# Square, value and score products in other groups: a decoder step on one core

## The chip, the cores and the metric

One core of a Trainium2 chip runs the kernel. The metric is the time of one execution on the device in microseconds (us). Matrix products run on TensorE (PE), and the other compute engines are VectorE (DVE), ScalarE (ACT) and GpSimd (POOL); SyncE (SP) issues most transfers. Each engine works through its own list of instructions in order, and waits on semaphores for the others.

## The reference

One inference step of a one-layer decoder over 512 prompt tokens and 8 samples of 4 tokens, 1024 wide, all in fp32. Cut to what matters:

```python
def rmsnorm(x, g):
    return x * rsqrt(mean(x * x, -1) + EPS) * g

# both groups
h = rmsnorm(x, norm_mix_g) @ w_in          # -> ua va | q k v | qi ki wi
a = gelu(ua) * (tril(gm_ws) @ layernorm(gelu(va)) + gm_bs)
# prompt: per query the 128 best of index_scores(qi, wi, ki), causal
# samples: the 256 best of 2048 cached tokens (pages of 128) and the 4 new ones
b = softmax(q @ k_sel.T / 8) @ v_sel
x = x + concat(a, b) @ w_out
x = x + mem_attend(rmsnorm(x, norm_mem_g), mk, mv) @ mem_wo
xn = rmsnorm(x, norm_ffn_g)
# experts: 8 heads, 16 best of 128 x 128 keys, chosen rows of two tables
x = x + sum(softmax(top16) * gelu(u_tab[eid] . xn) * v_tab[eid])
return rmsnorm(x, final_norm_g), ...       # and keys, values, memory keys and values
```

## The kernel before

Activations stand with features on the partitions: `xT[p, kt, token]`, eight tiles of 128 features. A weight product is made of three products in a rounded fp32 format (`mm3`, lines 249 to 251: high x high, high x low, low x high). The two parts of a weight tile are split by ACT (line 213, the cast) and DVE (line 217, the rest); the parts of an activation by lines 192 and 193.

The program goes through a front stage (first norm, projections `wA`, masks by sorting the indexing scores, prompt attention, the selection for the samples and their attention, the memory), then two halves of the tokens (256 prompt tokens, and 256 with the 32 sample tokens: 288 columns). Each half has `wO`, a norm, `wMQ`, memory attention, `wMO`, a norm, `wP`. In the trace the first half's wO ends about 350 us, the second half's wO runs from 402 to 440, wMO from 440 to 460 and from 515 to 540. The experts follow, from about 570 us.

The order of the instructions on each engine is that of a scheduler, which lays the program out by its own estimate of times; the program only names dependencies, priorities by order of writing, and `issue_after(x)`, under which what is written comes behind x.

Three places are edited.
- `squares4` (line 139) adds up the squares of a norm. ACT squares a tile (line 141); of every four tiles, tile c's columns are summed by a product with ones into partitions 32c to 32c+31 of an accumulator (line 147). It is called from `folded` (first norm, two accumulators, 272 columns each) and from `residual` (line 528), which adds an output tile to `xT` (line 527, DVE) and squares it. A norm needs eight products for each accumulator; the squares' buffers are four (`bufs=4`). Then `turned` and `row_factors` (lines 116 to 126 and 185 to 187) make the factors of the rows.
- `attend` has the prompt's attention in four blocks of 128 queries. `values` sums over b + 1 blocks of keys (line 886), for two groups of heads, which write partitions 0 to 63 and 64 to 127 of one bank.
- `sample_keys` multiplies each sample's queries with its cached keys (line 1496). Each page holds its keys in a 16-element slice per partition group; four slices (e), two pages (f), two halves of the rows (o, each with an accumulator of its own) and two halves of the output (c). ACT copies the accumulators (line 1500), and the next pages are fetched. The samples' value products are line 1553.

An fp32 product, as these three are, shows in the trace as two passes on PE.

Of the kernel before, what the change touches and what calls it, by code (L numbers as in the profile page):

```python
# [18 lines left out]
P = 128  # L19
NP = 512  # L20
NS = 32
NT = NP + NS
KT = 8
# [28 lines left out]
class Kernel:  # L52
# [83 lines left out]
                                  start=kt == 0 and b == 0, stop=kt == KT - 1, skip_group_check=True)  # L136


    def squares4(self, room, x, kt, st, w):
        sq = self.t(room, [P, w], tag="nsqs", bufs=4)  # L140
        self.nc.scalar.square(sq, x)
        self.sq4 = [sq] if kt % 4 == 0 else self.sq4 + [sq]
        if kt % 4 == 3:
            n = w // len(st)
            for i, ps in enumerate(st):
                for c, q in enumerate(self.sq4):
                    self.nc.tensor.matmul(ps[c * NS : c * NS + NS, :n], self.ones[:, :NS], q[:, i * n : i * n + n],
                                          start=kt == 3, stop=kt == KT - 1, skip_group_check=True)


    def turned(self, room, st, w):
# [693 lines left out]
    def attend(self, pw, qT, kT, v_n, mb):  # L845
        nc = self.nc
        keep = {}

        def scores(b, r):
            L = (b + 1) * P  # L850
            pss = [self.pst("pa") for g in range(2)]
            for g, ps in enumerate(pss):
                o = g * 64
                nc.tensor.matmul(ps[:, :L], qT[o : o + 64, r, b * P : b * P + P], kT[o : o + 64, :L], start=True, stop=True)
            return [soft(b, ps[:, :L]) for ps in pss]

        def soft(b, ps):
            sm = self.t(pw, [P, 512], tag="sm", bufs=2 * self.SKEW + 2)[:, : (b + 1) * P]
            mx = self.t(pw, [P, 1], tag="mx", bufs=4)
            nc.vector.tensor_tensor_reduce(sm, ps, mb[b], 0.125, NEG, ALU.add, ALU.max, mx)  # L860
            nm = self.t(pw, [P, 1], tag="nm", bufs=4)
            nc.vector.tensor_scalar(nm, mx, -1.0, None, ALU.mult)
            z = self.t(pw, [P, 1], tag="z", bufs=4)
            nc.scalar.activation(sm, sm, AF.Exp, bias=nm, accum_out=z)
            rz = self.t(pw, [P, 1], tag="rz", bufs=4)
            nc.vector.reciprocal(rz, z)
            nc.scalar.activation(sm, sm, AF.Copy, scale=rz)
            return sm

        def values(b, r, sms):  # L870
            L = (b + 1) * P
            if r == 0:
                keep["y"] = self.pst("pc")
            yb = keep["y"]
            for g, sm in enumerate(sms):
                if r % 2 == 0:
                    keep[g] = self.t(pw, [P, 4, 2, P], tag=f"pts{g}", bufs=self.PTB)
                pt = self.pst("pb")
                for s in range(b + 1):
                    nc.tensor.transpose(pt[:, s * P : s * P + P], sm[:, s * P : s * P + P], self.ident)  # L880
                nc.scalar.copy(keep[g][:, : b + 1, r % 2, :], pt[:, :L].rearrange("p (s t) -> p s t", t=P))
            if r % 2:

                for s in range(b + 1):
                    for g in range(2):
                        nc.tensor.matmul(yb[g * 64 : g * 64 + 64, (r - 1) * P : (r + 1) * P], v_n[:, s, g * 64 : g * 64 + 64],
                                         keep[g][:, s, :, :], start=s == 0, stop=s == b, skip_group_check=True)
            if r == 3:

                nc.scalar.copy(qT[:, :, b * P : b * P + P], yb.rearrange("p (r t) -> p r t", r=4))  # L890
                self.attended = b + 1


        ahead = []
        for b in range(4):
            while b > self.masked:
                yield 1.0
            for r in range(4):
                ahead.append((b, r, scores(b, r)))
                if len(ahead) > self.SKEW:  # L900
                    values(*ahead.pop(0))
                yield self.ATT * (b + 1) / 2
        for x in ahead:
            values(*x)
            yield self.ATT * 2
# [551 lines left out]
    def sample_keys(self, s1, s2):  # L1457
        nc = self.nc

        qb = self.s_qb = self.t(s2, [P, 8, 2, 4, 4])  # L1460
        nc.vector.memset(qb, 0.0)
        for g in range(2):
            r = slice(g * 64, g * 64 + 64)
            for q in range(4):
                nc.vector.tensor_scalar(qb[r, :, g, q], self.s_q[r, q].rearrange("p (b t) -> p b t", t=4), 0.125, None, ALU.mult)

        qs = self.t(s2, [P, 4, 8, 16])
        self.s_room = Room(qs.rearrange("p e b q -> p (e b q)"))
        ps = self.pst("pb")
        for e in range(4):  # L1470
            perm = self.t(s1, [P, P], tag="qst", bufs=2)
            nc.vector.tensor_copy(perm.rearrange("p (u g d) -> p u g d", u=4, g=2),
                                  self.ident.rearrange("p (g e d) -> p e g d", g=2, e=4)[:, e].unsqueeze(1).to_broadcast([P, 4, 2, 16]))
            nc.tensor.matmul(ps[:, e * P : e * P + P], perm, self.s_q.rearrange("p r t -> p (r t)"), start=True, stop=True)
        for e in range(4):
            nc.scalar.activation(qs[:, e].rearrange("p b (r t) -> p r b t", r=4), ps[:, e * P : e * P + P].rearrange("p (r b t) -> p r b t", r=4, b=8),
                                 AF.Copy, scale=0.125)

        own = self.t(s2, [P, 4])
        nc.vector.tensor_reduce(own, self.ident.rearrange("p (r c d) -> p c r d", r=2, d=16), AX.XY, ALU.add)  # L1480
        yield 1.0
        while not self.indexed:
            yield 1.0
        S = [self.t(s1, [P, 4, 512], tag="S8", bufs=2) for _ in range(2)]
        self.s_S = [S[b // 4][:, b % 4, :] for b in range(8)]
        for b in range(8):
            q4 = self.t(s2, [P, 4, 64], tag="q4", bufs=2)
            nc.vector.tensor_tensor(q4.rearrange("p e (c q) -> p e c q", c=4), qs[:, :, b].unsqueeze(2).to_broadcast([P, 4, 4, 16]),
                                    own.unsqueeze(1).unsqueeze(3).to_broadcast([P, 4, 4, 16]), ALU.mult)

            pair = [self.pst("pb") for _ in range(2)]
            for e in range(4):
                for f in range(2):
                    for o, ps in zip((0, 64), pair):
                        for c in range(2):
                            nc.tensor.matmul(ps[c * 64 : c * 64 + 64, f * P : f * P + P], q4[o : o + 64, e],
                                             self.kv[b][o : o + 64, 2 * c + f, e * P : e * P + P], start=e == 0 and f == 0, stop=e == 3,
                                             skip_group_check=True, tile_position=(o, c * 64))
            for r, ps in enumerate(pair):
                nc.scalar.copy(self.s_S[b].rearrange("p (m r f x) -> p r f m x", m=4, r=2, f=2)[:, r],  # L1500
                               ps[:, : 2 * P].rearrange("p (f m x) -> p f m x", f=2, m=4))
            self.fetch_kv(s2)
            yield 4.0 * self.SK
        self.keyed = True
# [366 lines left out]
```

## Time and profile before

| what | value |
|---|---|
| time, median of 3 (lowest to highest) | 1797.16 us (1795.39 to 1797.25) |
| the profiled execution: its time, its span | 1793.41 us, 1791.7 us |
| PE busy | 1675.7 us, 94% |
| DVE busy | 1482.9 us, 83% |
| ACT busy | 863.2 us, 48% |
| POOL busy | 503.6 us, 28% |
| PE in line 147 (96 passes), line 886 (80), line 1496 (512): median pass | 406, 380, 270 ns |

Busy is the time in which at least one instruction of the engine runs. A pass's own length contains the filling and draining of the array, which overlap the next one; so the distance from a start to the next start is what a pass costs. The shares are means over stages with different limits, and are to be read stage by stage.

### The profile page before, as it was taken

What the parts mean: (1) busy time and instruction counts of PE and PEld (TensorE: products, weight loads), DVE (VectorE), ACT (ScalarE), POOL (GpSimd) and SP (SyncE); (2) the same over time, 40 slices, a digit from 0 to 9 for tenths busy, and PEclk for the clock granted to TensorE, in tenths of its full rate; (3) what the DMA queues carried; (4) which work ended last, traced back from release to release, by engine and by line L of the source; (5) the groups of instructions that cost most, each with busy time, mean ns of one, the idle gap of its engine ahead of it and who ended that gap; (6) DMA issues with size and microseconds to landing.
All of it is one profiled execution on the core that took longest, in us unless ns stands there. A gap on an engine that the chain in (4) does not pass through costs nothing. (4 is left out here: it accounts for less than half of the span.)

```text
span 1791.7 us, 30106 instructions
## 1 busy us (share of the span) xinstructions
PE 1675.7 (94%) x10494; PEld 1476.6 (82%) x10494; DVE 1482.9 (83%) x3654; ACT 863.2 (48%) x1584; POOL 503.6 (28%) x437
## 2 busy tenths in 40 slices
PE   7999889989996999799999999999999999999995
PEld 5879757778875889789899998888788888888884
DVE  4586899755759999998999887799898888878897
ACT  4355765764543434674675575233343333333333
POOL 3000123120000054223224222334333534345343
PEclk9999769989998999999999999999999999999997
DMA  5423425445752599789779789799998999999986
GB/s 179 128 83 98 126 85 199 140 166 170 238 172 90 169 345 329 267 316 334 256 269 322 242 306 316 267 353 333 360 356 300 375 357 328 349 334 324 358 305 231
DMA packets 195207, 460.36 MB, mean 257 GB/s; under 512 B 17976, under 2 KB 98616, under 8 KB 193648
## 3 DMA queue, kind: packets, MB, share of 16 engines
q1 hardware_dynamic: 132928, 241.63, 39.7%
q0 software_dynamic: 53072, 207.71, 32.5%
q10 hardware_dynamic: 9056, 9.11, 1.6%
q8 instruction: 82, 1.34, 0.3%
q14 instruction: 69, 0.57, 0.1%
HBM read 416.11 MB, written 42.05 MB: 256 GB/s over the span
## 5 line engine op out<-in xcount | busy, mean ns | idle before, releaser
L251 PE MATMUL t<-t,t 128*128 128x384 f32 (+3 forms) x2544 | 867.9, 346 | 12.5 <-DVE t L217 12.2
L250 PE MATMUL t<-t,t 128*128 128x384 f32 (+3 forms) x2544 | 867.6, 343 | 0.0
L249 PE MATMUL t<-t,t 128*128 128x384 f32 (+3 forms) x2544 | 779.9, 346 | 17.6 <-ACT t L213 15.1
L213 ACT CAST t<-t 128x1024 fp32r<-128x1024 f32 (+4 forms) x512 | 418.2, 841 | 716.8 <-PE t L250 475.8
L217 DVE TENSOR_TENSOR t<-t,t 128x1024 fp32r<-128x1024 f32 (+4 forms) x512 | 488.6, 965 | 140.0 <-ACT t L213 136.3
L251 PEld LDWEIGHTS t<-t,t 128*128 128x128 f32 x2544 | 485.0, 191 | 66.4 <-DVE t L217 15.7
L249 PEld LDWEIGHTS t<-t,t 128*128 128x128 f32 x2544 | 485.0, 191 | 61.2 <-ACT t L213 20.3
L250 PEld LDWEIGHTS t<-t,t 128*128 128x128 f32 x2544 | 485.4, 191 | 38.4 <-issue 5.7
L1276 POOL DMA_INDIRECT t<-in_u,t x160 | 201.7, 1260 | 499.0 <-DVE t L1736 305.0
L1276 POOL DMA_INDIRECT t<-in_v,t x160 | 215.5, 1347 | 298.0 <-DVE t L1741 233.9
L1741 DVE SCALAR_TENSOR_TENSOR t<-t,t,t 128x1024 f32<-128x1024 f32 x160 | 204.9, 1281 | 4.5 <-DMA t<-in_v,t 3.6
L1736 DVE SCALAR_TENSOR_TENSOR t<-t,t 128x1024 f32<-128x1024 f32 x160 | 193.8, 1219 | 8.7 <-DMA t<-in_u,t 8.6
L1081 ACT ACTIVATE t<-t 128x512 f32<-128x512 f32 x96 | 96.6, 1148 | 19.3 <-DMA wd<-t 18.5
L1276 POOL DMA_INDIRECT t<-in_cK,t x32 | 32.3, 1009 | 212.1 <-PE t L1359 146.5
L1217 DVE TENSOR_TENSOR t<-t,t 128x352 f32<-128x352 f32 x128 | 66.6, 521 | 6.2 <-DMA t<-wd 4.0
L1097 ACT ACTIVATE t<-t 128x384 f32<-128x384 f32 x128 | 62.3, 487 | 11.8 <-PE t L251 9.2
L1071 ACT ACTIVATE t<-t,t 128x128 f16<-128x128 f16 x192 | 58.2, 395 | 10.1 <-DVE t L1067 7.4
L1078 PE MATMUL t<-t,t 128*128 128x128 f16 x384 | 51.8, 221 | 9.4 <-ACT t L1081 8.8
L1276 POOL DMA_INDIRECT t<-in_cV,t x32 | 34.2, 1069 | 72.0 <-PE t L1553 45.1
L695 ACT ACTIVATE t<-t,t 128x384 f32<-128x384 f32 x64 | 42.7, 666 | 24.4 <-DVE t L692 20.3
L1079 PE MATMUL t<-t,t 128*128 128x128 f16 x384 | 49.7, 221 | 0.4 <-DVE t L1073 0.3
L1079 PEld LDWEIGHTS <-t 128*128 128x128 f16 x384 | 36.7, 98 | 10.6 <-issue 10.1
(400 smaller groups left out, 1471.2 us busy)
## 6 DMA issues: line engine op xcount, KB each, us to landing
t<-in_uT SPq DMA_DIRECT2D x128, 512.0 KB, 5.8
t<-in_v SPq DMA_DIRECT2D x128, 512.0 KB, 6.2
wd<-t POOLq DMA_DIRECT2D x11, 2048.0 KB, 9.2
t<-wd SPq DMA_DIRECT2D x32, 704.0 KB, 7.9
gd<-t SPq DMA_DIRECT2D x56, 192.0 KB, 5.3
t<-gd SPq DMA_DIRECT2D x56, 192.0 KB, 7.6
t<-in_wA SPq DMA_DIRECT2D x19, 512.0 KB, 4.0
t<-in_wO SPq DMA_DIRECT2D x16, 512.0 KB, 4.0
```

The costliest lines, as they stand in the source:

```text
L213: self.nc.scalar.copy(hi, x)
L217: self.pin_v = self.nc.vector.tensor_tensor(lo, x, hi, ALU.subtract)
L249: mm(out, ah, bh, start=first, stop=False)
L250: mm(out, ah, bl, start=False, stop=False)
L251: self.pin = mm(out, al, bh, start=False, stop=last)
L1079: nc.tensor.matmul(o, oj[:, x, :], ol[:, x, :], start=False, stop=True)
L1081: nc.scalar.activation(wb[:, :, t : t + 4].rearrange("p i t -> p t i"), ps.rearrange("p (t i) -> p t i", t=4), AF.Copy, scale=1.0 / 2048.0)
L1097: nc.scalar.activation(G, ps, AF.Gelu_apprx_tanh)
L1217: nc.vector.tensor_tensor(q(w)[:, : 4 * NB - 1], self.wp[:, :, i % 4, :], q(G)[:, : 4 * NB - 1], ALU.mult)
L1276: self.nc.gpsimd.indirect_dma_start(out=out, out_offset=None, in_=src, in_offset=bass.IndirectOffsetOnAxis(ap=ix, axis=0))
L1736: nc.vector.scalar_tensor_tensor(r, r, 1.0, hf, ALU.mult, ALU.mult, accum_out=a[:, k : k + 1])
L1741: nc.vector.scalar_tensor_tensor(acc, r, a[:, k : k + 1], acc, ALU.mult, ALU.add)
```

## The change

`together` takes products written as functions. It issues the last of them first, and the others under `issue_after` of it. `squares4` hands it the four products of an accumulator, `values` the two products of one block of keys. In `sample_keys` the loop over f is gone: one product of 256 columns covers both pages, and the number of products falls from 256 to 128.

```diff
--- before.py
+++ after.py
@@ -136,6 +136,13 @@
                                   start=kt == 0 and b == 0, stop=kt == KT - 1, skip_group_check=True)
 
 
+    def together(self, products):
+        first = products[-1]()
+        with self.tc.issue_after(getattr(first, "ins", first)):
+            for p in products[:-1]:
+                p()
+
+
     def squares4(self, room, x, kt, st, w):
         sq = self.t(room, [P, w], tag="nsqs", bufs=4)
         self.nc.scalar.square(sq, x)
@@ -143,9 +150,9 @@
         if kt % 4 == 3:
             n = w // len(st)
             for i, ps in enumerate(st):
-                for c, q in enumerate(self.sq4):
-                    self.nc.tensor.matmul(ps[c * NS : c * NS + NS, :n], self.ones[:, :NS], q[:, i * n : i * n + n],
-                                          start=kt == 3, stop=kt == KT - 1, skip_group_check=True)
+                self.together([lambda c=c, q=q: self.nc.tensor.matmul(ps[c * NS : c * NS + NS, :n], self.ones[:, :NS], q[:, i * n : i * n + n],
+                                                                      start=kt == 3, stop=kt == KT - 1, skip_group_check=True)
+                               for c, q in enumerate(self.sq4)])
 
 
     def turned(self, room, st, w):
@@ -882,9 +889,9 @@
             if r % 2:
 
                 for s in range(b + 1):
-                    for g in range(2):
-                        nc.tensor.matmul(yb[g * 64 : g * 64 + 64, (r - 1) * P : (r + 1) * P], v_n[:, s, g * 64 : g * 64 + 64],
-                                         keep[g][:, s, :, :], start=s == 0, stop=s == b, skip_group_check=True)
+                    self.together([lambda g=g: nc.tensor.matmul(yb[g * 64 : g * 64 + 64, (r - 1) * P : (r + 1) * P], v_n[:, s, g * 64 : g * 64 + 64],
+                                                                keep[g][:, s, :, :], start=s == 0, stop=s == b, skip_group_check=True)
+                                   for g in range(2)])
             if r == 3:
 
                 nc.scalar.copy(qT[:, :, b * P : b * P + P], yb.rearrange("p (r t) -> p r t", r=4))
@@ -1490,12 +1497,11 @@
 
             pair = [self.pst("pb") for _ in range(2)]
             for e in range(4):
-                for f in range(2):
-                    for o, ps in zip((0, 64), pair):
-                        for c in range(2):
-                            nc.tensor.matmul(ps[c * 64 : c * 64 + 64, f * P : f * P + P], q4[o : o + 64, e],
-                                             self.kv[b][o : o + 64, 2 * c + f, e * P : e * P + P], start=e == 0 and f == 0, stop=e == 3,
-                                             skip_group_check=True, tile_position=(o, c * 64))
+                for o, ps in zip((0, 64), pair):
+                    for c in range(2):
+                        nc.tensor.matmul(ps[c * 64 : c * 64 + 64, : 2 * P].rearrange("p (f x) -> p f x", f=2), q4[o : o + 64, e],
+                                         self.kv[b][o : o + 64, 2 * c : 2 * c + 2, e * P : e * P + P], start=e == 0, stop=e == 3,
+                                         skip_group_check=True, tile_position=(o, c * 64))
             for r, ps in enumerate(pair):
                 nc.scalar.copy(self.s_S[b].rearrange("p (m r f x) -> p r f m x", m=4, r=2, f=2)[:, r],
                                ps[:, : 2 * P].rearrange("p (f m x) -> p f m x", f=2, m=4))
```

Lines behind 139 have numbers higher by 7 in the changed kernel (by 6 behind the score products): line 147 is 153, 886 is 892, 1496 is 1502, 249 to 251 are 256 to 258.

PE, the second half's wMO, where its last square product stands (t_6586 is the accumulator of the squares, t_58 the ones, t_7009 and t_7056 accumulators of the next weight tiles). Before:

```order
L251 MATMUL t_7009<-t_6768,t_7006 128x288
L249 MATMUL t_7009<-t_6768,t_7005 128x288
L249 MATMUL t_7056<-t_6768,t_7052 128x288
L250 MATMUL t_7056<-t_6769,t_7052 128x288
L250 MATMUL t_7009<-t_6769,t_7005 128x288
L251 MATMUL t_7009<-t_6768,t_7006 128x288
L147 MATMUL t_6586<-t_5273,t_58 32x288
L249 MATMUL t_7009<-t_6768,t_7005 128x288
L251 MATMUL t_7056<-t_6768,t_7053 128x288
```

Of the changed kernel (the accumulator of the squares is t_6458 here, the next weight tiles' are t_6881 and t_6928):

```order
L258 MATMUL t_6881<-t_6640,t_6878 128x288
L256 MATMUL t_6881<-t_6640,t_6877 128x288
L256 MATMUL t_6928<-t_6640,t_6924 128x288
L257 MATMUL t_6928<-t_6641,t_6924 128x288
L257 MATMUL t_6881<-t_6641,t_6877 128x288
L258 MATMUL t_6881<-t_6640,t_6878 128x288
L153 MATMUL t_6458<-t_5145,t_58 32x288 x4
L256 MATMUL t_6881<-t_6640,t_6877 128x288
L258 MATMUL t_6928<-t_6640,t_6925 128x288
L256 MATMUL t_6928<-t_6640,t_6924 128x288
```

The four products stand in one run at the place where the fourth stood alone; the other three had such places of their own, twelve weight products apart.

PE, the samples' scores between the prompt's second block of values (t_3403 and t_3404 are a sample's two accumulators, t_3198 the values'; t_3199 and t_3204 the two head groups' probabilities). Before:

```order
L854 MATMUL t_3444<-t_168,t_157 128x256
L854 MATMUL t_3445<-t_168,t_157 128x256
L1496 MATMUL t_3403<-t_2972,t_3401 64x128
L886 MATMUL t_3198<-t_3199,t_169 64x256
L1496 MATMUL t_3403<-t_2972,t_3401 64x128
L1496 MATMUL t_3404<-t_2972,t_3401 64x128 x2
L1496 MATMUL t_3403<-t_2972,t_3401 64x128 x2
L1496 MATMUL t_3404<-t_2972,t_3401 64x128 x2
L1496 MATMUL t_3403<-t_2972,t_3401 64x128
L886 MATMUL t_3198<-t_3204,t_169 64x256
L886 MATMUL t_3198<-t_3199,t_169 64x256
```

Of the changed kernel (accumulators t_3339 and t_3340, values t_3150):

```order
L861 MATMUL t_3364<-t_168,t_157 128x256
L861 MATMUL t_3365<-t_168,t_157 128x256
L1502 MATMUL t_3339<-t_2940,t_3337 64x256 x8
L1502 MATMUL t_3340<-t_2940,t_3337 64x256
L892 MATMUL t_3150<-t_3156,t_169 64x256
L892 MATMUL t_3150<-t_3151,t_169 64x256
L892 MATMUL t_3150<-t_3156,t_169 64x256
L892 MATMUL t_3150<-t_3151,t_169 64x256
L1502 MATMUL t_3340<-t_2940,t_3337 64x256 x7
L887 MATMUL t_3389<-t_60,t_3259 128x128 x2
```

The value products stand in pairs of the two head groups; the scores' products no longer alternate between the accumulators, but eight of the one stand before eight of the other.

DVE, the second half's last norm (t_6926 and t_6798 are the row factors, rows with MAX, MAX_INDEX and MATCH_REPLACE the experts' routing of the first token block). Before, around the factors' last step (line 126):

```order
L981 TENSOR_TENSOR t_7040<-t_6818 128x8x24
L126 TENSOR_TENSOR t_6926<-t_6920,t_6922 128x3
L981 TENSOR_TENSOR t_7040<-t_6818 128x8x16
L931 MAX t_6818<-t_6848 128x8
L928 MATCH_REPLACE t_6850<-t_6818,t_6793 128x128
L928 MATCH_REPLACE t_6852<-t_6818,t_6793 128x128
L928 MATCH_REPLACE t_6854<-t_6818,t_6793 128x128
L185 TENSOR_SCALAR t_6929<-t_60,t_6926 128x128
L185 TENSOR_SCALAR t_6932<-t_60,t_6926 128x128
L936 MAX_INDEX t_6819<-t_6818,t_6848 128x8
L931 MAX t_6818<-t_6850 128x8
```

Of the changed kernel, from the reciprocal root's first step (line 116) to behind its last:

```order
L116 TENSOR_SCALAR t_6788<-t_6784 128x3
L120 RECIPROCAL t_6792<-t_6790 128x3
L122 TENSOR_TENSOR t_6794<-t_6792 128x3
L123 TENSOR_TENSOR t_6794<-t_6794,t_6788 128x3
L124 TENSOR_SCALAR t_6794<-t_6794 128x3
L931 MAX t_6690<-t_6665 128x8 x4
L126 TENSOR_TENSOR t_6798<-t_6792,t_6794 128x3
L935 MATCH_REPLACE t_6696<-t_6690,t_6665 128x128
L940 MAX_INDEX t_6691<-t_6690,t_6665 128x8
L931 MAX t_6690<-t_6665 128x8 x2
```

The norm's small steps follow each other directly, where sorting stood between them, and the products' diagonal factors (line 185, now 192) come after fewer of the sort's rows.

## Rows read from the trace of the kernel before

**Rows 1.** The page, part 1: TensorE's busy time in us, its share of the span and its instructions (each pass of an fp32 product counts).

```profile
PE 1675.7 (94%) x10494; PEld 1476.6 (82%) x10494; DVE 1482.9 (83%) x3654; ACT 863.2 (48%) x1584; POOL 503.6 (28%) x437
```

**Rows 2.** The table of stretches: for each stretch (us from the span's start) its length, then the busy time of each engine with the number of its instructions, the granted TensorE clock as a share of full speed, the share of DMA time and GB/s.

```profile
251.00:290.00 39.00, 38.43 (x446) 32.15 (x446) 37.70 (x159) 23.87 (x60) 13.44 (x14) 0.95 0.47 150
290.00:333.00 43.00, 40.57 (x343) 32.49 (x342) 39.15 (x143) 24.65 (x49) 6.80 (x7) 1.00 0.49 160
333.00:384.00 51.00, 50.42 (x525) 39.88 (x524) 31.84 (x105) 38.88 (x88) 21.89 (x20) 1.00 0.57 187
402.00:440.00 38.00, 38.00 (x256) 32.89 (x255) 19.00 (x33) 17.84 (x33) 0.85 (x4) 1.00 0.53 184
440.00:460.00 20.00, 20.00 (x137) 16.24 (x136) 13.94 (x31) 12.59 (x31) 0.00 (x0) 1.00 0.58 185
...
515.00:540.00 25.00, 25.00 (x160) 19.93 (x159) 13.85 (x26) 13.79 (x26) 0.00 (x0) 1.00 0.61 198
540.00:570.00 30.00, 15.35 (x99) 14.27 (x98) 29.01 (x161) 8.84 (x18) 0.00 (x0) 0.72 0.21 66
```

**Rows 3.** The timeline of PE in the second half's wO (start, length, engine, line, operation, output<-inputs, partitions x columns, how many in the run). Between the last two rows stand 24 products of lines 249 to 251.

```profile
413.02 0.29 PE L250 MATMUL t<-t,t 128*128 128x288 f32 x1
413.24 0.68 PE L147 MATMUL t<-t,t 128*32 128x288 f32 x4
413.85 0.40 PE L251 MATMUL t<-t,t 128*128 128x288 f32 x1
414.09 0.30 PE L249 MATMUL t<-t,t 128*128 128x288 f32 x1
...
417.27 0.67 PE L147 MATMUL t<-t,t 128*32 128x288 f32 x2
```

**Rows 4.** The timeline of PE in wMO, two neighbouring runs of line 147 in the first half and two in the second half, with twelve products of lines 249 to 251 between the last two.

```profile
440.93 0.62 PE L147 MATMUL t<-t,t 128*32 128x256 f32 x2
...
443.22 0.62 PE L147 MATMUL t<-t,t 128*32 128x256 f32 x2
...
517.60 0.67 PE L147 MATMUL t<-t,t 128*32 128x288 f32 x2
...
520.01 0.67 PE L147 MATMUL t<-t,t 128*32 128x288 f32 x2
```

**Rows 5.** The timeline of PE in the first half's wO: a run of two square products (four passes), a run of the samples' value products (line 1553) and a run of one square product (two passes).

```profile
344.13 0.63 PE L147 MATMUL t<-t,t 128*32 128x256 f32 x4
...
345.70 1.08 PE L1553 MATMUL t<-t,t 128*32 128x128 f32 x32
...
349.21 0.62 PE L147 MATMUL t<-t,t 128*32 128x256 f32 x2
```

**Rows 6.** The timeline of PE: a lone value product at half clock, two runs of score products, then a lone value product at full clock and the row that follows it.

```profile
242.30 1.11 PE L886 MATMUL t<-t,t 128*64 128x256 f32 x2
...
256.98 3.22 PE L1496 MATMUL t<-t,t 64*64 64x128 f32 x62
...
285.78 1.43 PE L1496 MATMUL t<-t,t 64*64 64x128 f32 x44
...
354.71 0.65 PE L886 MATMUL t<-t,t 128*64 128x256 f32 x2
355.28 0.39 PE L251 MATMUL t<-t,t 128*128 128x256 f32 x1
```

**Rows 7.** The timeline of PE and, in the second row, of ACT at the kernel's start; then two pairs of neighbouring rows of PE, at half and at full clock.

```profile
10.30 5.86 PE L147 MATMUL t<-t,t 128*32 128x272 f32 x16 [10.30 <-ACT t L141]
...
13.72 0.64 ACT L141 ACTIVATE t<-t 128x544 f32<-128x544 f32 x1
...
251.57 0.41 PE L250 MATMUL t<-t,t 128*128 128x256 f32 x1
251.78 0.42 PE L251 MATMUL t<-t,t 128*128 128x256 f32 x1
...
255.08 0.28 PE L250 MATMUL t<-t,t 128*128 128x256 f32 x1
255.20 0.28 PE L251 MATMUL t<-t,t 128*128 128x256 f32 x1
```

**Rows 8.** The timeline of DVE at the second half's last norm: the first step of the reciprocal root (line 116), the reciprocal (line 120), the copy of the factors (line 187).

```profile
541.32 0.17 DVE L116 TENSOR_SCALAR t<-t 128x3 f32<-128x3 f32 x1
...
543.31 0.17 DVE L120 RECIPROCAL t<-t 128x3 f32<-128x3 f32 x1 [0.64 <-ACT t L118]
...
560.70 0.45 DVE L187 COPY t<-t 128x288 f32<-128x288 f32 x1
```

**Rows 9.** The groups by line of DVE from 517.60 to 529.66 us, five output tiles of the second half's wMO: count | busy us, mean ns | idle time before them and what ended it.

```profile
L217 DVE TENSOR_TENSOR t<-t,t 128x512 fp32r<-128x512 f32 x5 | 3.4, 689 | 0.3
L193 DVE SCALAR_TENSOR_TENSOR t<-t,t,t 128x288 fp32r<-128x288 f32 x6 | 3.1, 514 | 0.3
L527 DVE TENSOR_TENSOR t<-t,t 128x288 f32<-128x288 f32 x6 | 2.7, 455 | 3.4 <-PE t L251 3.4
```

**Rows 10.** The timeline of PE, three of the samples' eight value steps: the second, the third and the last.

```profile
351.84 1.08 PE L1553 MATMUL t<-t,t 128*32 128x128 f32 x32
...
362.23 0.97 PE L1553 MATMUL t<-t,t 128*32 128x128 f32 x28
...
384.39 1.08 PE L1553 MATMUL t<-t,t 128*32 128x128 f32 x32 [0.73 <-ACT t L1546]
```

## The prediction

> **What bounds the kernel now.** The page's first lines say that TensorE (PE) is busy 94% of the span [rows 1], but that is a mean over stages, so I read the table of stretches next [rows 2]. From 251 to 333 us PE works 79.0 of 82 us and VectorE (DVE) 76.9: the bit search for the samples' threshold runs on DVE there and both are full. From 333 to 460 us, and again from 515 to 540, PE is the only full engine: 50.42 of 51, 38.00 of 38, 20.00 of 20, 25.00 of 25, with DVE at 31.84, 19.00, 13.94, 13.85 and ScalarE (ACT) at 38.88, 17.84, 12.59, 13.79. There, and only there, a microsecond taken off PE is a microsecond off the kernel. From 540 to 570 us it is the reverse: PE has 15.35 of 30, DVE 29.01. Behind that the order of PE's work is also new up to about 1114 us, but none of the edited products is there.
>
> Then the timeline of PE says what one edited product costs. In the first stretch with w = 288 [rows 3], ordinary products follow each other every 0.134 us. The lone square product at 417.27 comes 4.03 us after the one before it, and between them stand 24 ordinary products: 24 x 0.134 = 3.22, so one interruption costs **0.81 us**. Its two passes (an fp32 product is two passes here) are about 0.48 us of that; the rest is lost on the way in and out (413.02 to 413.24 is 0.22 us, and 413.85 to 414.09 0.24, where 0.134 is usual). Where an output tile has half as many products [rows 4] it is the same: 2.41 us from 517.60 to 520.01, of which twelve products take 1.61, leaves **0.80**.
>
> The decisive view is what a second product costs that writes other output partitions [rows 5]. The run at 344.13 has four passes, two products, and is 0.63 us long; the run at 349.21 has one product and is 0.62. So the second was free. At 345.70 sixteen products in four groups of 32 partitions, 32 passes, end within 1.08 us, 0.03 us each. Four groups run side by side.
>
> **The change part by part.** *Squares of the residuals.* Four products that stood one by one now stand as one run of four. Each run that disappears is worth 0.80 us at w = 288 columns, and at w = 256 the 0.62 us of [rows 5] less the 0.07 that lies over the next product (413.24 + 0.68 against 413.85), plus 0.2 lost around it: 0.75. Lone or paired runs before, and runs after, by the order of the instructions: first wO (up to 350 us) 6 to 2, second wO (402 to 440) 7 to 2, first wMO (440 to 460) 8 to 2, second wMO (515 to 540) 8 to 2.
> - first wO: 4 x 0.75 = 3.0, half of it before 333 us and half behind.
> - second wO: 5 x 0.80 = **-4.0**. DVE and ACT have half the stretch free, so I take all.
> - second wMO: 6 x 0.80 = 4.8 for PE. But DVE works 3.4 + 3.1 + 2.7 = 9.2 us in the 12.06 us of five tiles [rows 9]; PE's ordinary products alone would need 8.05 there. So five tiles can give 12.06 - 9.2 = 2.9, and a little of the others: **-3.3**. Bounds 2 and 4.8.
> - first wMO: its period is 2.29 us [rows 4], 6 x 0.75 = 4.5 at most; the same brake: **-3.0**. Bounds 2 and 4.5.
>
> What waits anew: the fifth square of a norm now needs a buffer that the whole group frees, since there are four. The group stands where the fourth product stood, its length is about that of one, so ACT's queue (the casts of weights behind it) is held no longer than PE's 0.7 us, four times; the next square is 1.7 us away. I cost it at nothing; without that cover 4 x 0.7 = 2.8 us.
>
> *Attention values.* Six times (twice each for blocks 1 to 3) a lone product of 0.57 us from its start to the next [rows 6] (at 354.71), 0.77 with its way in and out, disappears into pairs; the run behind it keeps its number of pairs. Four of these stand before 333 us (3.1), two behind (1.5). Block 0's four lone runs at half clock, 1.1 us each [rows 6] (at 242.30), become two: 2.2.
>
> *Scores.* The number of streamed columns stays. What counts is how many positions of the array are in flight: 64 passes took 3.33 us where all of one accumulator stood before the other (two positions), 1.98 us where they alternated (four) [rows 6]. The new order has one accumulator's eight products before the other's for two samples that alternated, wholly or half: +1.35 and +0.65 us, less what the halved count of weight loads gives. I take **+1.6** (bounds: 2.0, and -1.5 if the two-position runs were held by their loads rather than their columns).
>
> So 240 to 333 us gives PE 2.2 + 3.1 + 1.5 - 1.6 = 5.2 us. DVE is just as full from 251 on and has only 82 - 76.9 = 5.1 us of air in that stretch; I take **-3.0**, a little over half (bounds -1 and -5.2). From 333 to 384 us: 1.5 + 1.5 = **-3.0**, PE alone being full.
>
> *Start.* All eight first products now wait for the fourth square, which ends at 13.72 + 0.64 = 14.36 us; before, the run from 10.30 was paced by the squares and ended at 16.16 [rows 7]. Two groups at the half-clock price of [rows 6] take 2 x 1.1 and end at 16.6: +0.4. PE is idle four us longer, and the granted clock may rise later: products of 256 columns follow each other every 0.21 us at half clock (1.2 GHz) where 0.12 is usual (2.4 GHz) [rows 7] (from 251.57 and from 255.08); some 25 products at the slower rate would be +2.3. I take **+0.4** (bounds 0 and 2.3).
>
> *Norm of the second half.* DVE's order moved: between the norm's first step and the copy of its factors stand 57 instructions instead of 75, the other 18 being the routing's sort steps. These 19.4 us [rows 8] hold 75, or 0.26 each: 4.7 us, less the wait for ACT's square root, which sorting covered before (the reciprocal behind it came 2.0 us after the first step) and which the new order leaves mostly open, 1.5: 3.2. The sort steps must still run, on an engine that is full: **-1.5** (bounds 0 and -3.2).
>
> Sum: +0.4 - 3.0 - 3.0 - 4.0 - 3.0 - 3.3 - 1.5 = **-17.4 us** against the profiled 1793.41. That execution lies 3.75 us under the median 1797.16; carried over to the median, 1797.2 - 17.4 = **1779.8 us**, -1.0%. From 570 us on I put nothing, with +-3 for the new order.
>
> **The rivals.**
> *B, everything passes.* DVE gives way as well: 5.2 + 3.0 + 4.0 + 4.5 + 4.8 + 3.2 - 0.4 = 24.3, **1773**. For it: PE is full in five stretches. Against: [rows 9].
> *C, PE's time is taken back by others.* If DVE rules up to 333 us, the samples' chain of gathers up to 384 and the split of weights in wMO, there remain 4.0 of wO and some 2.5 of wMO: **1790.5**. For it: DVE's 76.9 of 82.
> *D, slower: the samples' attention is pushed back.* In the new order its first product stands behind some fifty more ordinary products (50 x 0.12 = 6 us), and each of its eight steps needs pages that were gathered after an earlier step. The steps at 345.70, 351.84, 362.23 and so on to 384.39 [rows 5, 10] take 38.7 us, 5.5 each, the longest 10.4. Everything behind 402 us waits for the last one. Behind it 11.8 us are gained (4.0 + 3.0 + 3.3 + 1.5), and nothing ahead if the chain binds. From a mean step of (38.7 + 11.8) / 7 = 7.2 us it is no gain; at 8 us it is 56 - 38.7 - 11.8 = +5.5, **1803**. Against it: PE has filler between the steps, 50.42 of 51.
> *E, the four products don't overlap.* Then only the way in and out is saved, 0.81 - 0.48 = 0.33 for 21 square runs and six value runs, 8.9, with the norm's 1.5 and the losses of DVE's stretch and of scores (3 to 4): **1790**. Against it: the free second product of [rows 5].
> The Trainium skill's "TensorE: Matmul & The Clock Gate" (Part 3, The mechanism) speaks for E: weight loads are said to overlap running products only if they use other rows of the array, and these groups share all rows and differ in columns. The trace doesn't agree: two products took 0.63 us where one took 0.62.
>
> **How the numbers follow.** A (this forecast, 1774 to 1786) 0.52; B 0.20; C 0.16; E 0.05; D 0.07. A measurement tells 0.2%, 3.6 us, from no change. A, B, E and nearly all of C lie beyond that: faster 0.87; C's end and D's mild end are the same, 0.07; slower 0.06. The range 1766 to 1792 holds A, E, most of B and C; it leaves out D and B's bound with the -3 of the late order.
>
> **What would show it.** Right: square runs of eight passes, about 0.6 to 0.8 us long; 402 to 440 us shorter by 4; periods of 1.7 to 1.9 us in wMO, with DVE ending the waits; value runs of even pairs; score runs of 3.3 us for samples 4 and 5; the copy of the norm's factors 1 to 3 us nearer its first step. Wrong: a run of eight passes of over 1.5 us (E); new idle time of PE before the samples' value products (D); wO's gain given back at the wait before the experts (C). The forecast also fails if the new order behind 570 us moves PE's idle time there by much more than 3 us.

## The result and the profile after

The changed kernel takes 1782.01 us (median of 6, 1774.54 to 1789.20) against 1796.39 us (median of 6): ratio **0.9919**, 95% interval 0.9896 to 0.9943, or 14.4 us less. A second measurement of the same kernel gave 0.9913 (0.9885 to 0.9941). The profiled execution was the slowest of the six, 1789.20 us with a span of 1787.5; a second profile has a span of 1780.6. So the stretches are compared here, not the two spans.

The stretches ahead of the second half's wO, to be held against [rows 2] (same columns):

```profile
251.00:290.00 39.00, 39.00 (x321) 27.92 (x319) 36.35 (x149) 24.29 (x58) 17.08 (x16) 1.00 0.57 174
290.00:333.00 43.00, 40.78 (x330) 33.98 (x330) 40.97 (x152) 27.20 (x55) 5.21 (x5) 1.00 0.53 162
333.00:384.00 51.00, 45.25 (x456) 35.42 (x458) 28.90 (x98) 34.19 (x75) 19.85 (x20) 0.90 0.53 166
```

PE works 5 us less from 333 to 384 us than before and idles instead: 45.25 of 51, at a granted clock of 0.90 where there was 1.00. DVE has 40.97 of 43 from 290 to 333. The samples' attention does not end earlier for it (rows of the four places, below).

The timeline of PE, the answers to [rows 3, 4, 6]:

```profile
253.19 1.94 PE L1502 MATMUL t<-t,t 64*64 64x256 f32 x16
257.38 1.94 PE L1502 MATMUL t<-t,t 64*64 64x256 f32 x16
...
295.14 1.96 PE L1502 MATMUL t<-t,t 64*64 64x256 f32 x32
...
356.58 1.95 PE L892 MATMUL t<-t,t 128*64 128x256 f32 x16
...
422.87 0.69 PE L153 MATMUL t<-t,t 128*32 128x288 f32 x8
...
442.98 0.64 PE L153 MATMUL t<-t,t 128*32 128x256 f32 x8
...
527.45 0.69 PE L153 MATMUL t<-t,t 128*32 128x288 f32 x8
```

A group of eight passes takes 0.64 to 0.69 us, as a lone product did [rows 3, 5]. The value products stand in runs of four to sixteen passes (the row shown is one of sixteen), with no lone product ahead. A sample's scores take two runs of 1.94 us where one accumulator's products stand together and 1.96 us in all where they alternate: 0.12 us a pass in the one case, 0.06 in the other, columns and not loads.

Four places cut the program into stretches: the first product behind the samples' attention (line 1634, 1640 after), the last square product (147; 153), the last scaled tile of the last norm (586; 593), the first product of the second expert loop (1178; 1185). The rows of each line give minimum, median and maximum length in ns, then its first and last start in us. Before:

```profile
L1634 PE MATMUL t<-t,t x4: 275/385/422, 390.7 to 394.4; 128*128 128x128 f32 x4
L147 PE MATMUL t<-t,t x96: 378/406/663, 10.3 to 535.9; 128*32 128x272 f32 x32, 128*32 128x256 f32 x32, 128*32 128x288 f32 x32
L586 DVE SCALAR_TENSOR_TENSOR t<-t,t,t x16: 475/498/527, 468.5 to 582.0; 128x256 f32<-128x256 f32 x8, 128x288 f32<-128x288 f32 x8
L1178 PE MATMUL t<-t,t x48: 269/276/474, 1114.7 to 1129.4; 128*128 128x128 f32 x48
```

Of the changed kernel:

```profile
L1640 PE MATMUL t<-t,t x4: 421/422/554, 393.4 to 397.5; 128*128 128x128 f32 x4
L153 PE MATMUL t<-t,t x96: 378/406/662, 14.6 to 527.7; 128*32 128x272 f32 x32, 128*32 128x256 f32 x32, 128*32 128x288 f32 x32
L593 DVE SCALAR_TENSOR_TENSOR t<-t,t,t x16: 473/488/520, 464.3 to 567.6; 128x256 f32<-128x256 f32 x8, 128x288 f32<-128x288 f32 x8
L1185 PE MATMUL t<-t,t x48: 271/275/377, 1111.0 to 1125.2; 128*128 128x128 f32 x48
```

Before, the first product behind the samples starts at 390.7, and from there it is 145.2 us to the last square, 46.1 to the last scaled tile, 532.7 to the second expert loop, 677.0 to the end. In the changed kernel: 393.4, then 134.3, 39.9, 543.4 and 676.5.

### The profile page after: what moved, and what is told of

The parts are those of the page before. It is cut to its first block, busy times and chain, and to the rows that moved or that the text cites. A ratio compares the mean times of both kernels' runs of the same rounds, so it can differ in the third digit from the quotient of the medians.

```text
span 1787.5 us, 29611 instructions
## 1 busy us (share of the span) xinstructions
PE 1661.1 (93%) x10238; PEld 1465.2 (82%) x10238; DVE 1481.7 (83%) x3654; ACT 864.8 (48%) x1585; POOL 490.4 (27%) x437
## 4 chain that ended last, share of the span: by engine, by line
PE 66%; DVE 16%; issue 6%; ACT 4%; DMA 4%; SPq 1%; POOL 1%; POOLq 0%; DVEq 0%; ACTq 0%
PE t L256 20%; PE t L258 19%; PE t L257 19%; DVE t L224 3%; DVE t L1742 2%; DMA t<-in_uT 1%; ACT t L220 1%; POOL t L1283 1%; PE t L652 1%; DMA wd<-t 1%; DVE t L940 1%; SPq L1326 1%; DVE t L935 1%; DVE t L931 1%; DVE t L943 1%
## 5 line engine op out<-in xcount | busy, mean ns | idle before, releaser
L1283 POOL DMA_INDIRECT t<-in_u,t x160 | 194.3, 1215 | 506.3 <-DVE t L1742 261.3
L1283 POOL DMA_INDIRECT t<-in_v,t x160 | 208.9, 1306 | 305.7 <-DVE t L1747 237.8
```

Source lines behind the costliest of these rows:

```text
L1283: self.nc.gpsimd.indirect_dma_start(out=out, out_offset=None, in_=src, in_offset=bass.IndirectOffsetOnAxis(ap=ix, axis=0))
```

## The experiments

All were built from the kernel before, or from the changed one by taking parts back, so that they differ from before by the edits shown; the table has what each gave. Ratios are against the kernel before on the same chip, five rounds each (three for the last two); the stretches are those of one profiled execution, worked out from rows like the eight above. The profiled execution of before (1793.41 us) lies 2.3 to 5.6 us under the medians of before that were measured beside the experiments (1795.70 to 1799.01), so a row's stretches together can show less gain than its ratio.

| kernel | ratio (95%) | first product behind the samples, us | to last square | to last scaled tile | to second expert loop | to end |
|---|---|---|---|---|---|---|
| before | 1 | 390.7 | 145.2 | 46.1 | 532.7 | 677.0 |
| changed | 0.9919 (0.9896 to 0.9943) | 393.4 | 134.3 | 39.9 | 543.4 | 676.5 |
| changed, again | 0.9913 (0.9885 to 0.9941) | 390.7 | 134.1 | 40.0 | 537.4 | 678.4 |
| squares alone | 0.9901 (0.9873 to 0.9930) | 391.8 | 134.8 | 39.9 | 534.3 | 674.2 |
| values alone | 1.0041 (1.0025 to 1.0058) | 390.2 | 144.9 | 46.7 | 542.2 | 672.9 |
| scores alone | 0.9999 (0.9985 to 1.0014) | 391.2 | 145.4 | 47.0 | 535.4 | 675.9 |
| early norm | 1.0040 (1.0023 to 1.0056) | 391.9 | 145.2 | 27.7 | 558.9 | 675.6 |
| squares, early norm | 0.9965 (0.9950 to 0.9979) | 391.9 | 135.6 | 27.4 | 555.2 | 675.0 |
| squares and scores | 0.9922 (0.9901 to 0.9943) | 393.6 | 134.3 | 39.9 | 533.8 | 677.2 |
| squares and values | 0.9909 (0.9890 to 0.9929) | 391.3 | 134.2 | 39.9 | 539.5 | 675.7 |
| last wMO's squares alone | 0.9962 (0.9948 to 0.9976) | 393.2 | 141.9 | 40.4 | 540.7 | 673.3 |
| squares without last wMO | 0.9941 (0.9921 to 0.9962) | 392.7 | 137.7 | 46.7 | 536.2 | 674.1 |
| before, 16 search steps | 0.9960 (0.9945 to 0.9975) | 384.9 | 147.1 | 46.1 | 532.5 | 676.9 |
| changed, 16 search steps | 0.9835 (0.9810 to 0.9859) | 377.3 | 137.1 | 39.9 | 538.9 | 677.1 |

**One part of the change at a time.** Each kernel has one hunk of the change:

```diff
# squares alone
-                for c, q in enumerate(self.sq4):
-                    self.nc.tensor.matmul(...)
+                self.together([lambda c=c, q=q: self.nc.tensor.matmul(...) for c, q in enumerate(self.sq4)])
# values alone
-                    for g in range(2):
-                        nc.tensor.matmul(yb[...], ...)
+                    self.together([lambda g=g: nc.tensor.matmul(yb[...], ...) for g in range(2)])
# scores alone
-                for f in range(2):
-                    for o, ps in zip((0, 64), pair):
+                for o, ps in zip((0, 64), pair):
```

> Only squares4 hands its four products to together; values and scores as before. Theory S (the gain is the squares' alone, made behind the samples' chain): 14 to 18 us less than before, ratio 0.990 to 0.992; the second half's wO 4 us shorter, its wMO 4 us shorter, the last norm 4 to 6 us shorter; the first norm 1 to 2 us later. Rival V (values and scores carry half of it): 7 to 9 us less, 0.995 to 0.996.

> Only the attention's value products stand in pairs; squares and scores as before. Theory S: no gain, within 2 us of before (0.999 to 1.001), since DVE's bit search and not PE sets when the samples' attention starts; PE has 4 to 7 us less work before 384 us and as much more idle time. Rival V (PE alone is full there): 4.6 to 6.8 us less, 0.996 to 0.9975.

> Only the score products cover two pages each; squares and values as before. Theory S: within 2 us of before; two-position runs cost 3.3 to 3.9 us for a sample, four-position runs 2.0, as with 128 columns. Rival W (weight loads held them): two-position runs 1.7 us for a sample, and 1.5 us or more less in all.

> The changed kernel once more, for a second profile. Theory X (the stretch of the first experts, from the last half's norm to the end of the first expert weights, varies from execution to execution by what DVE, ACT and the transfers do there): 8 to 12 us between executions, and the stretch from 571 to 1111 us of the first profile, 539.7 us, is 530 to 538 here, with the time 1775 to 1785. Rival O (the new order costs 10 us there every time): 538 to 541 again, and the gain that is lost is lost by order.

Squares alone gave 0.9901: all of the gain, and theory S's number. One part of S missed: the first norm's factors were to come 1 to 2 us later, and are copied at 32.77 us where it was 33.60. Its rows of the four places:

```profile
L1641 PE MATMUL t<-t,t x4: 421/421/553, 391.8 to 395.9; 128*128 128x128 f32 x4
L153 PE MATMUL t<-t,t x96: 379/406/661, 14.5 to 526.6; 128*32 128x272 f32 x32, 128*32 128x256 f32 x32, 128*32 128x288 f32 x32
L593 DVE SCALAR_TENSOR_TENSOR t<-t,t,t x16: 475/486/509, 462.4 to 566.5; 128x256 f32<-128x256 f32 x8, 128x288 f32<-128x288 f32 x8
L1185 PE MATMUL t<-t,t x48: 270/275/377, 1100.8 to 1113.8; 128*128 128x128 f32 x48
```

Scores alone gave nothing, as S had it. The two runs of a sample with one accumulator each take 1.94 us apiece in this kernel too (252.98 and 255.48 us), where W had 1.7 for both, so W is out. Values alone were slower by 0.4%, which neither theory expected. The table says where not: up to the last scaled tile nothing moved by more than 0.7 us in any stretch. In the execution profiled the loss is in the first experts, 542.2 us for 532.7, of which it had 4.1 back by the end. What the pairs do on PE is seen in the sums of the engines' busy time from 209 to 390 us, first of the kernel before, then of values alone:

```profile
sum 181.00, PE 158.82 PEld 125.44 DVE 146.32 ACT 121.92 POOL 53.87; mean PE 52.94 PEld 41.81 DVE 48.77 ACT 40.64 POOL 17.96
sum 181.00, PE 154.67 PEld 125.19 DVE 146.88 ACT 119.69 POOL 56.04; mean PE 51.56 PEld 41.73 DVE 48.96 ACT 39.90 POOL 18.68
```

PE worked 4.2 us less and the stretch ended half a microsecond earlier; the rest is idle time of PE. So PE's work does not set the end of this stretch, as S had it, and the time is given away at the place where it was saved. That DVE's search sets the end, S's reason, is not shown by it.

The changed kernel's second profile had 537.4 us in the first experts, inside X's 530 to 538 (X counts from 571 us, some 4 us further on, and by that count it is 533.7); its first had 543.4. So part of that stretch changes from execution to execution, by 6 us between these two, less than the 8 to 12 that X had; but nearly all the changed kernels are above 532.7 there, so O is not out either.

**The last norm's order.** Routing steps are no longer written ahead of this one norm:

```diff
+            self.NORM = 0.0
             norm(2, *fold)
+            self.NORM = 12.0
```

> The kernel before with one number changed: no routing steps are written ahead of the second half's last norm (NORM 0 for this one norm, 12 us elsewhere), so that DVE's rows from the norm's first step to the copy of its factors are 10 and not 75. Theory N (part of the gain is the norm's earlier end, and DVE makes up for the sort steps later): 4 to 6 us less than before, ratio 0.9965 to 0.998, with the last scaled tile 5 to 9 us earlier behind the norm's first step. Rival T (DVE is full and takes it back before 1114 us): within 2 us of before.

> Squares grouped, values and scores as before, and no routing steps ahead of the last norm. Theory N: 2 to 4 us less than squares alone, ratio 0.987 to 0.989. Rival T: as squares alone, 0.990.

Theory N fell, and T was too kind as well: both kernels lost, 0.40% against before and 0.64% against squares alone. The last scaled tile, the start of the second expert loop and PE's largest wait from 560 to 1130 us (total, times, longest) in the kernel before with this edit:

```profile
L588 DVE SCALAR_TENSOR_TENSOR t<-t,t,t x16: 475/494/519, 469.7 to 564.8; 128x256 f32<-128x256 f32 x8, 128x288 f32<-128x288 f32 x8
L1180 PE MATMUL t<-t,t x48: 275/275/377, 1123.7 to 1135.6; 128*128 128x128 f32 x48
PE t L251 <- DVE t L217: 29.4, 21, 8.1
```

The norm and what hangs on it end 18 us sooner (27.7 for 46.1), and the first experts take 26 us longer (558.9 for 532.7). There PE waits 29.4 us for the experts' weight splits (line 217), which run on the same DVE as the sort steps that were put off, and 12.2 in the kernel before. Whether the 6 us that the changed kernel gains at this norm are paid back in the same way is not shown.

**Two parts at a time.**

> Squares grouped and scores of two pages; values as before. Theory S (scores are worth nothing): as squares alone, 0.989 to 0.991.

> Squares grouped and values in pairs; scores as before. Theory P (the pairs themselves cost, by what they do to the selection and the prompt's masks before 390 us): 4 to 7 us more than squares alone, 0.993 to 0.995, and the samples' last product 3 us later than in squares alone. Rival O (the loss of values alone lies in the order that the scheduler gave the first experts there): as squares alone or within 3 us of it, 0.989 to 0.992, samples' last product unmoved.

0.9922 and 0.9909: neither is told apart from squares alone. With the squares in place the pairs cost nothing that can be measured, so P is out. The 0.4% of values alone is then a matter of that kernel's order, as rival O of this experiment had it; which part of the order is open.

**Which squares.** A flag chooses the norms whose products are grouped:

```diff
-                self.together(products)
+                if self.grouped:
+                    self.together(products)
+                else:
+                    for p in products:
+                        p()
# in residual: self.grouped = k and mo          (last wMO alone; mo is set ahead of wMO)
# or:          self.grouped = not (k and mo)    (without last wMO, nor the first norm)
```

> Squares grouped in the second half's wMO alone; all else as before. Theory L (this one stage gives its own 4 us, and the order of the last norm, 57 instructions and not 75, comes with it and gives 6): from the samples' last product to the last square 141 us (before 145.2), from there to the last scaled tile 40 (before 46.1), in all 8 to 11 us less, ratio 0.994 to 0.9955. Rival T (the norm's 6 us are taken back among the first experts): 3 to 5 us less, 0.997 to 0.998.

> Squares grouped in both wO and in the first half's wMO, not in the first norm and not in the second half's wMO; all else as before. Theory L: 139 us from the samples' last product to the last square, 46 behind it, in all 6 to 8 us less, ratio 0.9955 to 0.9965. If squares grouped ahead of 390 us count as well: 8 to 10 us less.

The stage terms come out one by one: 145.2 to 141.9 us with the last wMO alone (3.3), 145.2 to 137.7 with the other two behind 390 us (7.5). And the last norm is 40 us with the last wMO grouped and 46 to 47 without it, in every kernel of the table but the two with the edit of the norm. So this gain of 6 is a consequence of that one wMO: with its squares grouped the scheduler lays out the norm's steps in another order. The ratio 0.9962 (6.9 us) lies between L and T: some of the 6 us is taken back. Without the last wMO it is 0.9941 (9.8 us), more than the 6 to 8 of L; the first product behind the samples does not come earlier there (392.7 us), so squares ahead of it do not explain the rest, which stays open.

**The bit search.** In both kernels the lower half of the bits is left out, so tokens are chosen more coarsely. The line stands in two searches, and both have the edit: the one for the samples, and the one for the masks of the prompt's last two blocks:

```diff
-        for bit in range(31, -1, -1):
+        for bit in range(31, 15, -1):
```

> The kernel before with 16 of the 32 steps of the bit search for the samples' threshold (the lower half of the bits is left out). Theory D (DVE's search sets when the samples' attention ends, so PE's saved time ahead of it is worth nothing): the samples' last product 15 to 35 us earlier than 390.7. Rival H (the search is hidden, and what holds the front is a mix of PE at half clock, the masks and the gathers): less than 8 us earlier.

> The changed kernel with 16 of the 32 steps of the bit search (the lower half of the bits is left out). Theory D: with the search shorter PE is the limit ahead of the samples' last product, and this kernel has it 4 to 7 us earlier than the kernel before with 16 steps; in all 18 to 22 us less than that kernel. Rival H: within 3 us of it at that product, and 12 to 16 us less in all.

The last step of the masks' search in the kernel before and in it with 16 steps; then the first product behind the samples, in the kernel before with 16 steps and its stretch from 251 to 333 us, then in the changed kernel with 16 steps:

```profile
L706 DVE TENSOR_TENSOR t<-t,t x1: 161/161/161, 245.8 to 245.8; 128x2 uint32<-128x2 uint32 x1
L706 DVE TENSOR_TENSOR t<-t,t x1: 141/141/141, 188.8 to 188.8; 128x2 uint32<-128x2 uint32 x1
L1634 PE MATMUL t<-t,t x4: 273/275/275, 384.9 to 386.5; 128*128 128x128 f32 x4
251.00:333.00 82.00, 79.95 (x810) 64.29 (x809) 48.99 (x163) 50.79 (x121) 24.66 (x24) 0.97 0.52 168
L1640 PE MATMUL t<-t,t x4: 272/275/275, 377.3 to 378.9; 128*128 128x128 f32 x4
251.00:333.00 82.00, 82.00 (x723) 63.34 (x726) 53.46 (x177) 54.21 (x126) 29.48 (x28) 1.00 0.59 181
```

With the searches halved DVE works 49 and 53 of 82 us instead of 76.9, and PE is full in the changed kernel, 82.00 of 82. Now the change is worth 7.6 us ahead of this product (384.9 to 377.3), a little over the 4 to 7 of D, and 21.9 in all (1791.70 to 1769.77 us), within D's 18 to 22. But in the kernel before the cut brought only 5.8 us, where D had 15 to 35 and H less than 8: there H was right. In the changed kernel the same cut brings 16.1, or 13.4 against the second profile. So PE's saved time ahead of this product counts once the searches are shorter. Which of the two searches held it back these runs can't say, since the masks are ready 57 us earlier too.

## Why the prediction was right, and where not

It said 1779.8 us, 1766 to 1792; 1782.0 was measured, and 1782.2 the second time. That the two lie 2.2 us apart is in part luck: one of its steps failed and two were mis-sized, in opposite directions.

- *One run of four costs as much as one product* (the decisive step): right. Eight passes take 0.69 us, a lone product took 0.67. Rival E is out. So is, for these products, the rule that the Trainium skill's "TensorE: Matmul & The Clock Gate" (Part 3, The mechanism) gave for it.
- *Second wO, both wMO, -10.3 us in sum*: right, 10.9 and 11.1 in the two profiles, 10.4 with squares alone. Singly 7.5 for wO and the first wMO (said 7.0), 3.3 for the last wMO (said 3.3). Of the brake by DVE that [rows 9] gave little is seen: in the changed kernel PE waits 0.49 us for line 224 (at 524.47 us), and its last wMO alone gives 4.0 us, from PE's start ahead of it to its last run of squares (513.19 to 535.65 us before, 509.01 to 527.45 now). The 9.2 us of DVE counted six steps each of lines 193 and 527 for five tiles; five each are 8.3, which leaves 3.8 us to give and not 2.9.
- *240 to 384 us, -6.0*: **wrong**. The step that failed is "From 333 to 384 us: ... PE alone being full", with the half of the stretch ahead that I gave to PE. The first product behind the samples starts 2.7 us later or at the same 390.7, not 6 earlier. The samples' first product in the kernel before, then it and two of their value steps in the changed kernel:

```profile
332.77 0.19 PE L1562 MATMUL t<-t,t 128*128 128x32 bf16 x1
...
339.69 0.21 PE L1568 MATMUL t<-t,t 128*128 128x32 bf16 x1 [1.98 <-DVE t L1460]
...
350.48 0.75 PE L1559 MATMUL t<-t,t 128*32 128x128 f32 x20
...
387.08 1.08 PE L1559 MATMUL t<-t,t 128*32 128x128 f32 x32 [0.73 <-ACT t L1552]
```

It now starts at 339.69, behind a wait for DVE's last step of the selection (line 1460), where it was 332.77 before. PE's 50.42 of 51 up to 384 us was full because PE had filler in hand, not because it set the pace: with values alone 4.2 us less work of PE moved the product behind the samples by 0.5 us. C said that others would take PE's time back; which of its two chains does it, DVE's search or the gathers, stays open. DVE's selection alone does not: here is its last step in the changed kernel, then in the one with squares and values.

```profile
L1460 DVE TENSOR_SCALAR t<-t x1: 173/173/173, 339.5 to 339.5; 128x32 bf16<-128x32 f32 x1
L1460 DVE TENSOR_SCALAR t<-t x1: 171/171/171, 326.6 to 326.6; 128x32 bf16<-128x32 f32 x1
```

These lie 12.9 us apart, and the products behind the samples only 2.1 (393.4 and 391.3). A push back as in D is seen too, 6.9 us at the samples' first product, though by DVE's later selection (329.7 us before) and not by products ahead of it on PE; and the steps closed up again: 345.70 to 384.39 was 38.7 us, 350.48 to 387.08 is 36.6.
- *Scores +1.6*: the size was right in kind (two positions 0.12 us a pass, four 0.06), and worth nothing in the kernel.
- *Start +0.4*: about right. The rows of the start, three of the kernel before and then those of the changed one:

```profile
16.09 0.39 PE L249 MATMUL t<-t,t 128*128 128x256 f32 x1
...
16.81 0.28 PE L250 MATMUL t<-t,t 128*128 128x256 f32 x1
16.92 0.28 PE L251 MATMUL t<-t,t 128*128 128x256 f32 x1
...
14.62 2.04 PE L153 MATMUL t<-t,t 128*32 128x272 f32 x16 [14.62 <-ACT t L148]
16.59 0.58 PE L256 MATMUL t<-t,t 128*128 128x256 f32 x1
...
19.59 0.41 PE L256 MATMUL t<-t,t 128*128 128x256 f32 x1
19.80 0.41 PE L257 MATMUL t<-t,t 128*128 128x256 f32 x1
...
21.73 0.28 PE L257 MATMUL t<-t,t 128*128 128x256 f32 x1
21.84 0.28 PE L258 MATMUL t<-t,t 128*128 128x256 f32 x1
```

The first ordinary product comes at 16.59 instead of 16.09, and products follow each other every 0.21 us up to about 20 us, where before it was 0.11 to 0.12 by 16.81: the granted clock rose later, as the upper bound had it. The first norm's factors are copied at 34.46 us in this profile and 32.50 in the second, 33.60 before, so the delay is taken back or nearly so.
- *Last norm -1.5*: **mis-sized**, 6.2 here and 5.7 to 6.2 in the other kernels that have the new order; outside my bounds. Two terms were wrong. DVE's first step, reciprocal and copy of the factors in the changed kernel:

```profile
532.59 0.17 DVE L116 TENSOR_SCALAR t<-t 128x3 f32<-128x3 f32 x1
533.03 0.17 DVE L120 RECIPROCAL t<-t 128x3 f32<-128x3 f32 x1 [0.27 <-ACT t L118]
...
547.29 0.45 DVE L194 COPY t<-t 128x288 f32<-128x288 f32 x1
```

From the first step to the copy of the factors it was 19.38 us [rows 8] and is 14.70: 4.7 less, which is the whole of what I had counted for the sort steps. I took 1.5 us off it for the wait for ACT's root; the reciprocal now starts 0.44 us after the first step, with 0.27 of waiting. ACT shows why, in the kernel before and then in the changed one:

```profile
541.78 1.28 ACT L118 ACT_TABLE_LOAD   x1
543.08 0.20 ACT L118 ACTIVATE t<-t 128x3 f32<-128x3 f32 x1
...
531.20 1.28 ACT L118 ACT_TABLE_LOAD   x1
532.80 0.20 ACT L118 ACTIVATE t<-t 128x3 f32<-128x3 f32 x1 [0.32 <-DVE t L116]
```

The root needs its table, 1.28 us. Before, ACT loaded it at 541.78, behind a copy of the routing's scores and after DVE's first step (541.32 [rows 8]); now it is loaded at 531.20, ahead of that step (532.59). So the wait that I had left in place went too. And the giving back, which I booked here, is not found here.
- *Nothing from 570 us on, +-3*: **mis-sized**. The first experts took 10.7 and 4.7 us longer in the two profiles, 1.6 with squares alone. PE's largest wait there, in the kernel before from 560 to 1130 us and in the changed one (total, times, longest):

```profile
PE t L251 <- DVE t L217: 12.2, 7, 3.0
PE t L258 <- DVE t L224: 21.4, 13, 7.9
```

The longest ends at 720 us, where DVE does four steps of the experts' first table (line 1742) ahead of the split for which PE waits:

```profile
710.87 1.20 DVE L1742 SCALAR_TENSOR_TENSOR t<-t,t 128x1024 f32<-128x1024 f32 x1
...
717.62 1.21 DVE L1742 SCALAR_TENSOR_TENSOR t<-t,t 128x1024 f32<-128x1024 f32 x1
...
718.76 1.22 DVE L224 TENSOR_TENSOR t<-t,t 128x1024 fp32r<-128x1024 f32 x1
```

This wait does not by itself make the stretch long: with squares alone it is 22.7 us in all, and the stretch is 534.3.

So -10.3 was right, -6.0 was 0 to +2.7, -1.5 was -6.2, and 0 was +5 to +11. The last two cancel in part; that they are linked is likely by the experiment with the norm, but not shown for this kernel. By the two profiles all stretches together gain 4.2 and 11.1 us and not 14.4: the execution of before that was profiled lies 3.0 us under its median, those of the changed kernel 7.2 and 0.1 above theirs. How much of the loss among the first experts is the sort steps put off and how much the scheduler's other choices there is open: kernels with the long norm have 532.5 to 542.2 us, kernels with the short one 533.8 to 543.4.

## What to carry to other kernels

Small products that write different partition groups of one bank cost one when they stand next to each other; a scheduler that issues each as it becomes ready spreads them, and each then interrupts the stream for 0.8 us. Count such a saving only where PE sets the pace: a stretch in which PE is full of filler, but something else sets the end, gives the time back as idle time. When an order is made by a scheduler, allow for stretches that the edit doesn't touch: the first experts took 532.5 to 543.4 us in the twelve profiles with the norm's order left to itself. And book what a full engine puts off where it must be done.

## What the runs showed of the hardware that was not expected

Nothing of the array was new beyond the prices above. The scatter of single executions was larger than the three of before let expect: the changed kernel's six lie 14.7 us apart, and the kernel before, 3.8 us in its six beside them, spreads over 11.6 to 15.4 us in the 22 to 24 measured beside the experiments. Between the changed kernel's two profiles 6 us of the difference stand in the first experts and 2.7 ahead of the product behind the samples' attention.
